# A decoder trunk on one core: the first MLP's scale and shift loaded one channel tile at a time, in four pieces

## The chip, the cores and the metric

The kernel runs on one core of one Trainium2 chip. The core has five engines with an instruction queue each: TensorE (PE) multiplies matrices into PSUM, VectorE (DVE) and ScalarE (ACT) work on vectors, GpSimd (POOL) does almost nothing here, and SyncE (SP) issues nearly all transfers from memory. Instructions of one engine start in the order in which they stand in its queue; engines wait for each other by semaphores. The metric is the device time of one execution in microseconds (us), lower is better.

## The reference, cut to what matters

```python
D_MODEL, SEQ, DEPTH, D_FF = 1024, 256, 2, 4096

def modulate(h, shift, scale):
    return h * (1 + scale[:, None, :]) + shift[:, None, :]

def squared_relu_mlp(h, w_up, w_down):
    a = jax.nn.relu(h @ w_up)
    return (a * a) @ w_down

c_act = jax.nn.silu(c)
for i in range(DEPTH):
    mod = c_act @ w_mod[i] + b_mod[i]                 # 1024 -> 6 * 1024
    sh1, sc1, g1, sh2, sc2, g2 = jnp.split(mod, 6, axis=-1)
    h = modulate(rmsnorm(x, norm_mix[i]), sh1, sc1)
    y = pool_mixer(...) if i == 0 else moba_attention(...)
    x = x + g1[:, None, :] * y
    h = modulate(rmsnorm(x, norm_mlp[i]), sh2, sc2)   # the change: sh2 and sc2 of layer 0
    x = x + g2[:, None, :] * squared_relu_mlp(h, w_up[i], w_down[i])
return rmsnorm(x, norm_final)
```

All arithmetic is float32. The shift `sh2` and the scale `sc2` of layer 0 have 1024 values each, and each value is a product of the 1024 numbers `c_act` with a column of `w_mod[0]`: 8 MB of weights are read for these two vectors.

## The kernel before, in words

Channels lie on the 128 partitions, so 1024 channels are 8 **channel tiles** k = 0 to 7, and the residual is kept as `xs[k]`, 128 by 256. The two layers run one after the other; the change touches the first MLP (names `m0u` for up, `m0d` for down) and the work just ahead of it.

**The up projection.** It has 32 outputs n by 8 inputs k, 256 weight tiles of 128 by 128. A load of 1 MB, `raw_w_j`, brings 16 tiles (128 by 2048 numbers), and is used in two **halves** of 8 tiles. Half h is split into two rounded parts so that a product keeps float32 accuracy: ScalarE rounds it (`split_hi`, line 247, `w_hi`), VectorE subtracts (`split_lo`, line 252, `w_lo`). Four buffers hold the halves, so half h + 4 waits for TensorE to be done with half h. A tile is three matmuls: `w_hi` by the high input, `w_hi` by the low input, `w_lo` by the high input (lines 271, 272, 273). For the first 14 outputs the order is input by input (`UP_ORDER`, `G_UP0 = 14`): 14 tiles for k = 0, then 14 for k = 1, and so on, 112 tiles in all, tile numbers 0 to 111. After them come the 18 other outputs, tiles 112 to 255. Tiles 0 to 7 are issued together (`mm_sums`, line 279).

**The inputs.** Input k is `h01_k`: `u` is the residual times the gain `gs01` (from the scale) times the row norm (line 648, VectorE), the high part is `u` plus the shift, rounded (line 654, ScalarE), the low part is the rest (line 657, VectorE). The gain needs the scale of tile k, the high part its shift.

**Scale and shift.** They come in two ways. *By TensorE* (`pair_mm`, `take`): the loaded weights are the moving operand and `c_act` the weights, and VectorE picks the wanted column out of PSUM (`pair_out`, line 325, output `pk`). *By VectorE* (`mod_dve`, line 295): the transposed weights are multiplied by the row `cact` and summed along the row into one column, 1024 wide, one instruction a channel tile. Before, `mlp0` brings scale and shift of tiles 0 and 1 ahead of the first MLP matmul (2 MB, by TensorE). The later scale tiles come in pairs by VectorE (`("m", 0, 4, j)`), the shift of tiles 2 to 5 by TensorE (`shift1`, `shift2`), that of tiles 6 and 7 by VectorE. Each pair gives two inputs at once.

**What sets the order.** The program is recorded in the order of the Python code. `load_order` lists the transfers, `issue` emits the next of them, each time a buffer was used up. All of these loads share five buffers of 1 MB (`raw`). A second ring of 32 buffers of 256 KB (tag `al`) holds temporaries of the first mixer and then the up projection's outputs. `head(d, ...)` puts work in front of tile d of the up projection: the splits of halves 2 to 11 and the inputs of the later pairs stand there by hand. From half 12 on, `next_tile` splits half h + 3 in front of tile 8h.

**Ahead of the MLP**, the gate of the first mixer (`g10`, the last of its weights) lets `pool_out` finish the residual, squares are summed on TensorE (`pool_sum`, line 390), `n1.rstd` makes the norm on ScalarE and VectorE, `take("mlp0", 0)` and `take("mlp0", 1)` follow, `R1` spreads the norm, and `keep_warm` puts matmuls with unused results in between.

Of the kernel before, what the change touches and what calls it, by code (L numbers as in the profile page):

```python
# [139 lines left out]
def tile_hybrid_pool_moba(  # L140
# [127 lines left out]

# [33 lines left out]

    def pair_mm(name, i, region):
# [3 lines left out]
        cols = slice(0, 64) if whole else slice(0, P)  # L309
        for k in range(nk):  # L310
            c0 = k if whole else i * nk + k
            for q in range(4):
                nc.tensor.matmul(
                    region[32 * q : 32 * q + 32, cols], ccol[:, c0 : c0 + 1].to_broadcast([P, 32]), w[:, k, q],
                    start=c0 == 0, stop=c0 == KD - 1, skip_group_check=True,
                )
        issue()

    def pair_out(name, i, region):
        key = PAIRS[name][i]  # L320
        layer, m, j = key
        base = 0 if name in BY_VECTOR else 64 * i
        for a in range(2):
            t = tmp.tile([P, 32], F32, tag="pk", bufs=4, name="pk")
            nc.vector.scalar_tensor_tensor(
                t, region[:, base + a * 32 : base + (a + 1) * 32], mod_bias(*key)[:, a : a + 1], pick,
                op0=ALU.add, op1=ALU.mult, accum_out=mods[layer, m][:, 2 * j + a : 2 * j + a + 1],
            )
        known.add(key)

    def mod(*key):
        for a in range(2):
            mod_dve(key, a)
            yield
# [842 lines left out]
```

## Time and profile before

| | us |
|---|---|
| median of three runs | 546.38 (546.02 to 546.96) |
| the profiled execution, its own time | 546.91 |
| its span in the profile | 545.1 |
| first matmul of the first MLP (from the span's start) | 52.27 |
| first matmul of its down projection | 145.8 |

Busy shares of the span: PE 98%, DVE 76%, ACT 59%. The profile is one execution; its time is 0.53 us above the median, and its span leaves 1.8 us of that time outside. A busy share says how long instructions of an engine were under way. Times below count from the start of the span.

### The profile page before, as it was taken

The page shows a single profiled execution, that of the slowest core. Times are in us where ns is not written, and L with a number is a line of the kernel's source. Part 1 is how long each engine was busy: PE and PEld are TensorE (multiplying, and loading weights), DVE is VectorE, ACT ScalarE, POOL GpSimd, SP SyncE. Part 2 cuts the span into 40 slices and gives each one's busy share as a digit, 9 for nine tenths or more (in the row PEclk, how much of TensorE's full clock was granted, in tenths as well). Part 3 has the DMA queues.
Part 4 walks back from the last instruction along what each step waited for, and adds up shares of the span by engine and source line. Part 5 has one row for each costly group of instructions (what it writes and reads, how often), then busy time and mean ns, then how long its engine had stood idle before and what let it go on. Part 6 is the DMA issues. An engine that isn't in the chain of part 4 may idle for free.

```text
span 545.1 us, 10988 instructions
## 1 busy us (share of the span) xinstructions
PE 533.8 (98%) x4424; PEld 496.4 (91%) x4424; DVE 413.1 (76%) x834; ACT 323.9 (59%) x605; POOL 2.5 (0%) x18
## 2 busy tenths in 40 slices
PE   8989999999999999999999999999999999999995
PEld 7767999999988888999999999999999998888895
DVE  1856997799889889957999994777887786765541
ACT  4224427789644455446988777666988774445531
POOL 1000000000000000000000000000000000000000
PEclk9998999999999999999999999999999999999998
DMA  8999999468999989964567874344555567576002
GB/s 330 416 419 415 388 393 361 156 243 313 331 354 409 382 315 343 337 228 151 217 213 285 290 286 171 124 188 154 167 222 182 206 231 265 219 266 255 0 1 77
DMA packets 22338, 140.41 MB, mean 258 GB/s; under 512 B 2416, under 2 KB 4608, under 8 KB 5904
## 3 DMA queue, kind: packets, MB, share of 16 engines
q1 hardware_dynamic: 22048, 138.61, 68.0%
q10 hardware_dynamic: 144, 1.05, 0.5%
q8 instruction: 34, 0.56, 0.4%
q14 instruction: 16, 0.13, 0.1%
q0 software_dynamic: 96, 0.06, 0.0%
HBM read 138.64 MB, written 1.07 MB: 256 GB/s over the span
## 4 chain that ended last, share of the span: by engine, by line
PE 87%; DMA 6%; DVE 3%; ACT 2%; issue 1%; DVEq 0%; ACTq 0%
PE m1d L264 9%; PE m0d L264 9%; PE m0u L271 5%; PE m0u L273 5%; PE m0u L272 5%; PE m1u L271 5%; PE m1u L272 5%; PE m1u L273 5%; PE m0d L265 5%; PE m1d L265 5%; PE qkv L271 5%; PE qkv L272 4%; PE qkv L273 4%; DMA raw_c_sh<-in_w_mod 3%; DMA raw_c_g<-in_w_mod 3%; PE sc L940 1%
## 5 line engine op out<-in xcount | busy, mean ns | idle before, releaser
L252 DVE TENSOR_TENSOR w_lo<-raw_w,w_hi 128x1024 fp32r<-128x1024 f32 x160 | 194.5, 1223 | 60.5 <-ACT w_hi L247 58.8
L247 ACT CAST w_hi<-raw_w 128x1024 fp32r<-128x1024 f32 x160 | 166.6, 1047 | 80.1 <-PE m1d L264 24.7
L264 PE MATMUL m1d<-m1u_al,w_hi 128*128 128x512 f32 x224 | 78.2, 393 | 0.0
L264 PE MATMUL m0d<-m0u_al,w_hi 128*128 128x512 f32 x224 | 78.0, 392 | 0.0
L295 DVE SCALAR_TENSOR_TENSOR raw_m<-raw_m,cact 128x1024 f32<-128x1024 f32 x64 | 77.6, 1217 | 0.0
L271 PE MATMUL m1u<-h_raw,w_hi 128*128 128x258 f32 x256 | 72.8, 284 | 0.0
L272 PE MATMUL m1u<-h_raw,w_hi 128*128 128x256 f32 x256 | 72.6, 284 | 0.0
L273 PE MATMUL m1u<-h_raw,w_lo 128*128 128x258 f32 x256 | 72.5, 283 | 0.0
L271 PE MATMUL m0u<-h,w_hi 128*128 128x256 f32 x248 | 69.7, 281 | 0.0
L273 PE MATMUL m0u<-h,w_lo 128*128 128x256 f32 x248 | 69.5, 280 | 0.0
L272 PE MATMUL m0u<-h,w_hi 128*128 128x256 f32 x248 | 69.3, 280 | 0.0
L265 PE MATMUL m1d<-m1u_al,w_lo 128*128 128x256 f32 x224 | 62.8, 280 | 0.0
L265 PE MATMUL m0d<-m0u_al,w_lo 128*128 128x256 f32 x224 | 62.7, 280 | 0.0
L271 PE MATMUL qkv<-h_raw,w_hi 128*128 128x258 f32 x192 | 57.4, 299 | 0.0
L272 PE MATMUL qkv<-h_raw,w_hi 128*128 128x256 f32 x192 | 54.6, 284 | 0.0
L273 PE MATMUL qkv<-h_raw,w_lo 128*128 128x258 f32 x192 | 54.4, 284 | 0.0
L264 PEld LDWEIGHTS m1d<-m1u_al,w_hi 128*128 128x128 f32 x224 | 42.1, 188 | 9.6
L264 PEld LDWEIGHTS m0d<-m0u_al,w_hi 128*128 128x128 f32 x224 | 42.0, 188 | 9.4
L273 PEld LDWEIGHTS m1u<-h_raw,w_lo 128*128 128x128 f32 x256 | 48.8, 191 | 0.0
L271 PEld LDWEIGHTS m1u<-h_raw,w_hi 128*128 128x128 f32 x256 | 48.7, 190 | 0.0
L272 PEld LDWEIGHTS m1u<-h_raw,w_hi 128*128 128x128 f32 x256 | 48.5, 190 | 0.0
L271 PEld LDWEIGHTS m0u<-h,w_hi 128*128 128x128 f32 x248 | 46.7, 188 | 0.6 <-issue 0.4
(182 smaller groups left out, 989.2 us busy)
## 6 DMA issues: line engine op xcount, KB each, us to landing
raw_w<-in_w_all SPq DMA_DIRECT2D x79, 1024.0 KB, 5.6
raw_m<-in_w_mod SPq DMA_DIRECT2D x32, 1024.0 KB, 6.4
raw_c_sh<-in_w_mod SPq DMA_DIRECT2D x8, 1024.0 KB, 13.8
raw_c_g<-in_w_mod SPq DMA_DIRECT2D x4, 1024.0 KB, 13.5
raw_c_mlp<-in_w_mod SPq DMA_DIRECT2D x2, 1024.0 KB, 11.6
raw_c_shift<-in_w_mod SPq DMA_DIRECT2D x2, 1024.0 KB, 8.0
T<-bd SPq DMA_DIRECT2D x8, 256.0 KB, 10.0
x<-in_xT ACTq DMA_DIRECT2D x1, 1024.0 KB, 5.9
```

The source lines that it names most:

```text
L247: nc.scalar.copy(hi, raw)
L252: nc.vector.tensor_sub(lo, raw, hi.bitcast(F32))
L264: nc.tensor.matmul(b, hi, hl[:, : 2 * S], start=start, stop=False)
L265: nc.tensor.matmul(b[:, S:], lo, hl[:, :S], start=False, stop=stop)
L271: nc.tensor.matmul(dst, hi, xh, start=start, stop=False)
L272: nc.tensor.matmul(dst[:, :S], hi, xl, start=False, stop=False)
L273: nc.tensor.matmul(dst, lo, xh, start=False, stop=stop)
L295: nc.vector.scalar_tensor_tensor(raw[:, a], raw[:, a], 1.0, cact, op0=ALU.mult, op1=ALU.mult, accum_out=dst[:, a : a + 1])
L940: nc.tensor.matmul(self.sc[e][:, t * P : t * P + n], self.qk[rows, 0, t * P : (t + 1) * P], self.qk[rows, 1, S - n :], start=True, stop=True,)
```

## The change

The scale and the shift of one channel tile k are now one load of 1 MB, the chunk `ml` k: 128 scale values and 128 shift values. It is not loaded into one of the five `raw` buffers but as four pieces of 128 by 512 (256 KB each) into four of the `al` buffers. The loads alternate: chunk k, then weight load k. Chunks 0, 1 and 4 are packed for TensorE (`ML_PE`, `take_ml`), the five others for VectorE (`ml_dve`): four row sums of 512, two for the scale and two for the shift, then an addition of the halves of each, then the bias. The inputs are made one at a time (`Input(k)`), and `head_work` places their parts and the splits of halves 1 to 17 by a rule in place of the list by hand. The code's line numbers shift: after the change the parts of a weight tile are made in lines 251 and 256, `u` in 681, the high part in 686, the low part in 690, the row sums in 302, and the three matmuls of a tile are in lines 274 to 276. In the head, `fold(7, 5)` and `pool_sum(7)` move behind `pool_out(0)`.

```diff
-PAIRS |= {f"mlp{j}": ((0, 4, j), (0, 3, j)) for j in range(1)}
-PAIRS |= {f"shift{j}": ((0, 3, j),) for j in (1, 2)}
...
+ML = ((0, 3), (0, 4))
+ML_PIECES = 4
+ML_SLOT = [16 + k if k < 4 else 8 + k for k in range(KD)]
+ML_PE = (0, 1, 4)
...
-HEAD_STEPS = 12
+HEAD_STEPS = 18
...
-    pair("mlp0")
-    order.extend([("w0a",), ("w0b",), ("w", 1)])
-    order.extend([("m", 0, 4, 1), ("c", "shift1", 0), ("w", 2), ("w", 3), ("m", 0, 4, 2), ("c", "shift2", 0)])
-    order.extend([("w", 4), ("m", 0, 4, 3), ("m", 0, 3, 3), ("w", 5)])
+    order.extend([("ml", 0), ("w0a",), ("w0b",)])
+    for k in range(1, KD):
+        order.append(("ml", k))
+        order.append(("w", k))
+    order.append(("w", KD))
...
+        elif key[0] == "ml":
+            n = TPC * P // ML_PIECES
+            t = [al_tile([P, n], f"ml{key[1]}_{i}") for i in range(ML_PIECES)]
+            for i in range(ML_PIECES):
+                nc.sync.dma_start(t[i], w_mod[0, ML_SLOT[key[1]]][:, i * n : (i + 1) * n])
...
+    def row_sum(raw, act_row, out):
+        nc.vector.scalar_tensor_tensor(raw, raw, 1.0, act_row, op0=ALU.mult, op1=ALU.mult, accum_out=out)
...
+    def ml_dve(k):
+        h = ML_PIECES // 2
+        n = D // h
+        t = tmp.tile([P, 2, h], F32, tag="ml", name=f"mlsum{k}")
+        for i, raw in enumerate(loaded["ml", k]):
+            a, b = divmod(i, h)
+            row_sum(raw, cact[:, b * n : (b + 1) * n], t[:, a, b : b + 1])
+        nc.vector.tensor_add(t[:, :, 0], t[:, :, 0], t[:, :, 1])
+        bias = vec[:, V_BMOD + ML[0][1] * KD : V_BMOD + (ML[0][1] + 2) * KD].rearrange("p (a b) -> p a b", a=2)
+        nc.vector.tensor_add(both_ml[:, :, k], t[:, :, 0], bias[:, :, k])
+        known.update(m + (k,) for m in ML)
...
+    def take_ml(k):
+        n = KD // ML_PIECES
+        for i, t in enumerate(loaded["ml", k]):
+            w = t.rearrange("p (k q n) -> p k q n", k=n, q=4)
+            columns_mm(w, i * n, 64, n, region[f"ml{k}"], i == 0, i == ML_PIECES - 1)
...
     pool_out(1)
-    fold(7, 5)
     take("g10", 1)
     given("g10", 1)
     pool_out(0)
-    pool_sum(7)
+    fold(7, 5)
     keep_warm(1)
     pool_sum(3)
     pool_sum(2)
+    keep_warm(1)
+    pool_sum(7)
     pool_sum(1)
...
-    take("mlp0", 0)
-    take("mlp0", 1)
-    both_given("mlp0")
+    take_ml(0)
+    ml_given(0)
...
-    head(2, splits(2))
-    head(6, splits(3))
-    head(7, mods_of(4, 1))
-    head(14, take_late("shift1", 0), lambda: given("shift1", 0), inputs(1))
-    head(18, splits(4))
...
+    def head_work():
+        ins = {k: Input(k) for k in range(1, KD)}
+        order = sorted(
+            [(G_UP0 * k, "in", k) for k in range(1, KD)] + [(HALF * h, "w", h) for h in range(1, HEAD_STEPS)]
+        )
+        highs = []
+        held = []
+
+        def give(k):
+            if k in ML_PE:
+                ml_given(k)
+            else:
+                ml_dve(k)
+            ins[k].gain()
+            ins[k].scaled(R1)
+
+        for need, kind, x in order:
+            at = need - HALF + 1 - max(0, 4 * (x - 13))
+            if kind == "in":
+                if x in ML_PE:
+
+                    at = max(at, HALF)
+                    head(max(at - 5, HALF), lambda x=x: region.update({f"ml{x}": bank(f"pm{x}")[:, :P]}), lambda x=x: take_ml(x))
+                if held:
+                    head(at, held.pop())
+                head(at, lambda x=x: give(x))
+                if x in ML_PE:
+                    head(at, ins[x].high, ins[x].low)
+                else:
+                    highs.append(ins[x].high)
+                    held.append(ins[x].low)
+            else:
+                def both(x=x, highs=tuple(highs)):
+                    w = split_hi(x)
+                    for high in highs:
+                        high()
+                    split_lo(x, *w)
+
+                highs.clear()
+
+                head(43 if x == 7 else at, both)
+                if held:
+                    head(at, held.pop())
+        assert not held
```

Three places in the queues show it. In the rows, `h01_u2` is `u` of input 2, `h01_2` its low part, `w4_lo` the low part of weight half 4, and numbers behind a name are the buffers'.

VectorE around input 2, before: halves 2 and 3, the sums of the scale of tiles 2 and 3, their shift from PSUM, both inputs, then half 4.

```order
L252 TENSOR_TENSOR w2_lo_728<-raw_w_1_567,w2_hi_726 128x1024
L252 TENSOR_TENSOR w3_lo_734<-raw_w_1_567,w3_hi_732 128x1024
L295 SCALAR_TENSOR_TENSOR raw_m_0_4_1_615,mod0_4_118<-raw_m_0_4_1_615,cact_107 128x1024 x2
L299 TENSOR_TENSOR mod0_4_118<-mod0_4_118,vec_80 128x2
L325 SCALAR_TENSOR_TENSOR pk_824,mod0_3_117<-pmc_789,vec_80 128x32
L325 SCALAR_TENSOR_TENSOR pk_826,mod0_3_117<-pmc_789,vec_80 128x32
L358 SCALAR_TENSOR_TENSOR gs0_4_696<-mod0_4_118,vec_80 128x2
L648 SCALAR_TENSOR_TENSOR h01_u2_829<-x_82,gs0_4_696,n1_R_717 128x256
L648 SCALAR_TENSOR_TENSOR h01_u3_831<-x_82,gs0_4_696,n1_R_717 128x256
L657 SCALAR_TENSOR_TENSOR h01_2_833<-h01_u2_829,mod0_3_117,h01_2_833 128x256
L657 SCALAR_TENSOR_TENSOR h01_3_835<-h01_u3_831,mod0_3_117,h01_3_835 128x256
L252 TENSOR_TENSOR w4_lo_853<-raw_w_2_686,w4_hi_851 128x1024
```

VectorE at the same place after the change.

```order
L256 TENSOR_TENSOR w2_lo_847<-raw_w_1_494,w2_hi_845 128x1024
L256 TENSOR_TENSOR w3_lo_877<-raw_w_1_494,w3_hi_875 128x1024
L302 SCALAR_TENSOR_TENSOR ml2_0_496,mlsum2_901<-ml2_0_496,cact_107 128x512
L302 SCALAR_TENSOR_TENSOR ml2_1_497,mlsum2_901<-ml2_1_497,cact_107 128x512
L302 SCALAR_TENSOR_TENSOR ml2_2_498,mlsum2_901<-ml2_2_498,cact_107 128x512
L302 SCALAR_TENSOR_TENSOR ml2_3_499,mlsum2_901<-ml2_3_499,cact_107 128x512
L321 TENSOR_TENSOR mlsum2_901<-mlsum2_901 128x2
L323 TENSOR_TENSOR both_ml_126<-mlsum2_901,vec_80 128x2
L377 SCALAR_TENSOR_TENSOR gs0_4_738<-both_ml_126,vec_80 128x1
L681 SCALAR_TENSOR_TENSOR h01_u2_909<-x_82,gs0_4_738,n1_R_754 128x256
L256 TENSOR_TENSOR w4_lo_927<-raw_w_2_529,w4_hi_923 128x1024
L690 SCALAR_TENSOR_TENSOR h01_2_925<-h01_u2_909,both_ml_126,h01_2_925 128x256
```

One input takes the place of two, four sums of 512 and two additions that of two sums of 1024, one addition and the two picked columns, and half 4 now stands between `u` and the low part of input 2; input 3 has a group of its own, later.

TensorE from the last gate weights (`raw_c_g`) to the two unused products ahead of the first MLP matmul, before.

```order
L313 MATMUL pma<-raw_c_g_1_412,ccol 32x64 x32
L390 MATMUL n_rms<-ones,n_sq_521 128x1 x2
L343 MATMUL junk<-fill 128x256
L390 MATMUL n_rms<-ones,n_sq_577 128x1 x2
L390 MATMUL n_rms<-ones,n_sq_580 128x1 x2
L390 MATMUL n_rms<-ones,n_sq_623 128x1 x2
L390 MATMUL n_rms<-ones,n_sq_626 128x1 x2
L343 MATMUL junk<-fill 128x256
L313 MATMUL pmb<-raw_c_mlp_0_432,ccol 32x128 x16
L313 MATMUL pmb<-raw_c_mlp_1_476,ccol 32x128 x16
L411 MATMUL n_rms<-vec,n_r 128x128 x2
L343 MATMUL junk_700<-fill 128x256 x2
```

TensorE at the same place after the change.

```order
L362 MATMUL junk<-fill 128x256
L409 MATMUL n_rms<-ones,n_sq_618 128x1 x2
L409 MATMUL n_rms<-ones,n_sq_621 128x1 x2
L362 MATMUL junk<-fill 128x256
L409 MATMUL n_rms<-ones,n_sq_554 128x1 x2
L409 MATMUL n_rms<-ones,n_sq_671 128x1 x2
L409 MATMUL n_rms<-ones,n_sq_674 128x1 x2
L362 MATMUL junk<-fill 128x256
L331 MATMUL pmb<-ml_0_415,ccol 32x64 x8
L331 MATMUL pmb<-ml_1_416,ccol 32x64 x8
L331 MATMUL pmb<-ml_2_417,ccol 32x64 x8
L331 MATMUL pmb<-ml_3_418,ccol 32x64 x8
```

The scale and shift products are half as wide (64 columns in place of 128, in four pieces of 8), the sum of tile 7 (`n_sq_521`, now `n_sq_554`) moved behind those of tiles 3 and 2, and one more unused product stands there.

SyncE's transfers from the MLP's first modulation weights on, before.

```order
L204 DMA raw_c_mlp0_0_432<-in_w_mod 128x2048
L204 DMA raw_c_mlp0_1_476<-in_w_mod 128x2048
L193 DMA raw_w_0_503<-in_w_all 128x1024
L196 DMA raw_w_0_503<-in_w_all 128x1024
L204 DMA raw_w_1_567<-in_w_all 128x2048
L204 DMA raw_m_0_4_1_615<-in_w_mod 128x2048
L204 DMA raw_c_shift1_0_668<-in_w_mod 128x2048
L204 DMA raw_w_2_686<-in_w_all 128x2048
L204 DMA raw_w_3_723<-in_w_all 128x2048
```

SyncE's transfers at the same place after the change.

```order
L200 DMA ml0_0_415<-in_w_mod 128x512
L200 DMA ml0_1_416<-in_w_mod 128x512
L200 DMA ml0_2_417<-in_w_mod 128x512
L200 DMA ml0_3_418<-in_w_mod 128x512
L192 DMA raw_w_0_441<-in_w_all 128x1024
L195 DMA raw_w_0_441<-in_w_all 128x1024
L200 DMA ml1_0_444<-in_w_mod 128x512
L200 DMA ml1_1_445<-in_w_mod 128x512
L200 DMA ml1_2_446<-in_w_mod 128x512
L200 DMA ml1_3_447<-in_w_mod 128x512
L208 DMA raw_w_1_494<-in_w_all 128x2048
L200 DMA ml2_0_496<-in_w_mod 128x512
```

Chunk 0 (1 MB) stands where `mlp0` (2 MB) stood, so the first weights follow 1 MB earlier, and from there on chunks and weight loads alternate.

## Rows read from the trace of the kernel before

**Rows 1.** Stretches: length, busy PE, PEld, DVE, ACT, POOL; PEclk, DMA share, GB/s.
```profile
0.00:52.20 52.20, 47.36 (x662) 37.74 (x662) 27.67 (x119) 15.75 (x32) 1.99 (x17) 0.97 0.98 394
52.20:545.10 492.90, 486.49 (x3762) 458.62 (x3762) 385.43 (x715) 308.16 (x575) 0.49 (x1) 1.00 0.66 243
```

**Rows 2.** Chain that ended last, 46 to 52 us: start, duration (us), what.
```profile
46.20 0.54 PE junk L343 x2
46.73 3.49 PE pmb L313 x64
...
50.24 0.77 DVE pk L325 x8
...
51.19 0.49 DVE h_u L648
...
51.71 0.52 ACT h L654
...
52.27 3.14 PE m0u L279 x24
```

**Rows 3.** Two stretches of 1 us before the first MLP matmul (PEclk: granted clock).
```profile
49.00:50.00 1.00, 1.00 (x24) 0.73 (x16) 0.00 (x0) 0.00 (x0) 0.00 (x0) 0.50 0.97 393
50.00:51.00 1.00, 1.00 (x10) 0.85 (x7) 0.76 (x9) 0.00 (x0) 0.00 (x0) 0.88 1.00 401
```

**Rows 4.** TensorE timeline (ninth tile, late take), then the down projection's first group.
```profile
55.25 0.28 PE L271 MATMUL m0u<-h,w_hi 128*128 128x256 f32 x1
...
57.57 1.10 PE L313 MATMUL pmc<-raw_c_shift,ccol 128*32 128x64 f32 x64
...
L264 PE MATMUL m0d<-m0u_al,w_hi x224: 387/392/402, 145.8 to 223.5; 128*128 128x512 f32 x112
```

**Rows 5.** VectorE timeline: start, duration (us), line, operation, out<-in, shape.
```profile
34.94 0.69 DVE L502 SCALAR_TENSOR_TENSOR pd<-win,ph 128x512 f32<-128x512 f32 x1
35.55 0.15 DVE L506 TENSOR_TENSOR pe<-win,vec 128x2 f32<-128x2 f32 x1
...
46.60 0.15 DVE L402 RECIPROCAL n_y<-n_s 128x2 f32<-128x2 f32 x1
46.79 0.16 DVE L404 TENSOR_TENSOR n_q<-n_y 128x2 f32<-128x2 f32 x1
...
54.19 3.49 DVE L252 TENSOR_TENSOR w_lo<-raw_w,w_hi 128x1024 fp32r<-128x1024 f32 x3
...
58.74 1.22 DVE L295 SCALAR_TENSOR_TENSOR raw_m<-raw_m,cact 128x1024 f32<-128x1024 f32 x1
...
60.00 0.16 DVE L299 TENSOR_TENSOR mod<-mod,vec 128x2 f32<-128x2 f32 x1
...
60.42 0.16 DVE L358 SCALAR_TENSOR_TENSOR gs<-mod,vec 128x2 f32<-128x2 f32 x1
60.61 0.88 DVE L648 SCALAR_TENSOR_TENSOR h_u<-x,gs,n_R 128x256 f32<-128x256 f32 x2
61.68 0.89 DVE L657 SCALAR_TENSOR_TENSOR h<-h_u,mod,h 128x256 fp32r<-128x256 f32 x2 [0.19 <-ACT h L654]
```

**Rows 6.** Costliest groups on the page: ScalarE's rounding of the weights.
```profile
L247 ACT CAST w_hi<-raw_w 128x1024 fp32r<-128x1024 f32 x160 | 166.6, 1047 | 80.1 <-PE m1d L264 24.7
```

**Rows 7.** VectorE: halves 18 and 24 of the weights; then a stretch of 10 us.
```profile
98.68 1.23 DVE L252 TENSOR_TENSOR w_lo<-raw_w,w_hi 128x1024 fp32r<-128x1024 f32 x1 [1.58 <-ACT w_hi L247]
...
120.75 1.22 DVE L252 TENSOR_TENSOR w_lo<-raw_w,w_hi 128x1024 fp32r<-128x1024 f32 x1
...
120.00:130.00 10.00, 10.00 (x87) 10.00 (x87) 9.72 (x17) 9.84 (x21) 0.00 (x0) 1.00 0.84 301
```

**Rows 8.** DMA: 4 us of the head; then issues: KB each, median us to landing.
```profile
36.00:40.00 4.00, 3.66 (x70) 2.64 (x72) 2.10 (x13) 0.77 (x2) 0.00 (x0) 1.00 1.00 418
...
wp<-in_w_pool SPq DMA_DIRECT2D x4, 256.0 KB, 14.3
...
out<-y SPq DMA_DIRECT2D x4, 256.0 KB, 2.4
```

More of the change, by code (lines that the diff above doesn't have):

```diff
@@ L308, in pair_mm, with picked @@
         w = loaded["c", name, i].rearrange("p (k q n) -> p k q n", k=nk, q=4)
[L309 to L316, printed above, removed]
-        issue()
+        columns_mm(w, 0 if whole else i * nk, 64 if whole else P, nk, region, whole or i == 0, whole or i == 1)
+        issue()
+    def picked(region, base, out):
+        t = tmp.tile([P, 32], F32, tag="pk", bufs=4, name="pk")
+        nc.vector.scalar_tensor_tensor(
+            t, region[:, base : base + 32], mod_bias(*out), pick, op0=ALU.add, op1=ALU.mult, accum_out=mod_col(*out)
+        )
+        known.add(out)
     def pair_out(name, i, region):
-        key = PAIRS[name][i]
-        layer, m, j = key
-        base = 0 if name in BY_VECTOR else 64 * i
+        layer, m, j = PAIRS[name][i]
         for a in range(2):
[L324 to L334, printed above, removed]
+            picked(region, (0 if name in BY_VECTOR else 64 * i) + 32 * a, (layer, m, 2 * j + a))
     junk = [bank("junk")]
@@ L355, in gain @@
     def gain(layer, m, v0, g, j0=0, j1=KD):
-        assert all((layer, m, j) in known for j in range(j0 // 2, j1 // 2))
+        assert all((layer, m, j) in known for j in range(j0, j1))
         v = v0 + layer * KD
@@ L362, in modv @@
     def modv(layer, m, k=None):
-        assert all((layer, m, j) in known for j in (range(4) if k is None else (k // 2,))), (layer, m)
+        assert all((layer, m, j) in known for j in (range(KD) if k is None else (k,))), (layer, m)
         return mods[layer, m]
@@ L548, in both_given, with ml_given @@
             given(name, i)
+    def take_ml(k):
[3 more added lines that the diff above has]
+            columns_mm(w, i * n, 64, n, region[f"ml{k}"], i == 0, i == ML_PIECES - 1)
+    def ml_given(k):
+        for a in range(2):
+            picked(region[f"ml{k}"], 32 * a, ML[a] + (k,))
     rms.rstd()
@@ L828, in head @@
         later(d, run)
-    def mods_of(m, j):
-        return lambda: weave(mod(0, m, j))
-    def splits(*hs):
-        return lambda: [split(h) for h in hs]
-    def take_late(name, half):
-        def run():
-            if name not in region:
-                region[name] = bank("pmc")[:, :P]
-            take(name, half)
-        return run
-    def inputs(j):
-        return lambda: Input(j).all(R1)
     first = Input(0)
@@ L1119, with by_tile @@
     wm = asf(by_row)
+    def by_tile(m, k):
+        return w_mod[0][:, m * D + k * P : m * D + (k + 1) * P]
+    for k, slot in enumerate(ML_SLOT):
+        both = np.concatenate([by_tile(m, k) for _, m in ML], axis=1)
+        if k in ML_PE:
+            wm[0, slot] = both.reshape(KD, P, 2, 4, 32).transpose(1, 0, 3, 2, 4).reshape(P, 2 * D)
+        else:
+            wm[0, slot] = both.T.reshape(2, P, D).transpose(1, 0, 2).reshape(P, 2 * D)
     for name, keys in PAIRS.items():
```

102 lines of the change are left out of this document (47 added, 55 removed).

## The prediction

> **What bounds the kernel now.** I read the busy times by stretch first. Behind 52.2 us TensorE is busy 486.5 of 492.9 us, and transfers take 0.66 of the engines' time; ahead of it transfers are saturated (share 0.98) [rows 1]. So the program is a head that loads modulation weights, then one long run of matmuls: what moves the end is when that run starts, and whether a matmul in it waits. The chain of waits gives the start: the last unused product behind the sums of squares (46.20), the `mlp0` products (46.73, 3.49 us), four picked columns (0.77), `u`, the high part, first MLP matmul at 52.27 [rows 2]. From tile 8 on the matmuls follow each other: tile 8 starts at 55.25, the down projection at 145.8, two late products of 1.1 us lie between, so a tile takes (145.8 - 55.25 - 2.2)/248 = 0.356 us, and 14 tiles, one input's worth, 4.98 us [rows 4]. TensorE therefore sets a pace of 4.98 us an input and 2.85 us a weight half. The other view to read is VectorE's timeline, for its work must keep that pace and it starts its instructions strictly in the order of its queue.
>
> **Head.** `take_ml(0)` has half as many columns to pass through TensorE: 3.49/2 = 1.75 us in place of 3.49, at the halved clock (0.50, the 1.2 GHz level) under which `mlp0` ran [rows 2, 3]. Bounds: 1.1 us, as the same shape took at full clock [rows 4], and 2.2, twice that. Two picks in place of four save 0.38. The moved fold and sum give nothing by my reckoning: the three sums that stand last still need the last square, and one more unused product stands in a gap. So the products start at 46.73 as before and end at 48.48; two picks, 0.39, and then 1.25 us as between 51.02 and 52.27 give the first MLP matmul at 50.1, **-2.1 us** (-1.65 to -2.75). The first weight half must be rounded by then: it lands 1 MB, 2.5 us at 418 GB/s, earlier [rows 8], and its subtraction stands ahead of the low part, a wait below 0.1 us.
>
> **Transfers.** The bytes are the same 8 MB, in an order that alternates. At 418 GB/s a chunk and a weight load land every 5.0 us, from chunk 1 at some 49 us: chunk k lands about 5 us before its input is due, and the ring of 32 buffers is free by then (its old tiles belong to the first mixer, done by 46.2). I cost the pieces at nothing. A 256 KB load among the 1 MB loads of the head took 14.3 us from issue to landing, nearly all of it waiting in line, while the rate stayed at 418 GB/s; one alone took 2.4 us [rows 8]. The Trainium skill ("DMA: Bandwidth & Descriptors", Anatomy of one DMA) gives each transfer a fixed 2.0 us besides its bytes, for the software path; paid in full by every piece that would be 4 x 2.6 us a chunk. The rate in line speaks against paying it here, and the rival below prices it.
>
> **VectorE's load an input.** Prices [rows 5]: an operation 512 wide lasts 0.69 us and the next starts 0.61 after it (34.94, 35.55); a subtraction of a half lasts 1.22 and holds the queue 1.14 (three in 3.49); `u` and low part 0.49 each, 0.40 apart; a small operation that needs the one before starts 0.20 after it (46.60, 46.79), and `u` 0.19 after the gain (60.42, 60.61); an addition starts 0.04 after the sum's end (58.74 + 1.22, 60.00). The row sum of 512 isn't in the trace; the product of 512 at line 502, same operation and width without the sum, is the nearest row, and at 1024 the sum (1.22) costs what the subtraction costs, so I take 0.61. By VectorE an input then costs: three sums 1.83; the fourth's end and the addition 0.73; bias, gain and `u` 0.20 + 0.20 + 0.19; `u` 0.40; a half 1.14; the low part with what follows it 0.45; the second half 1.14: **6.3 us against TensorE's 4.98**. I walked the queues with a half's rounding at 1.05 us on ScalarE [rows 6] and get 6.37 with the hand-overs. Before, a pair (9.96 us of TensorE) costs at most two scale and two shift sums (4.6), four halves (4.6) and 2.5 for the inputs: 11.7 once, 9.4 for the pairs whose shift TensorE makes, with halves 1 to 3 and inputs 0 and 1 done before the pace begins. Now only input 0 is there.
>
> **Walk from 50.15** (time of the wait on TensorE, then what it waits for). Input 1: chunk products end at 54.2, `u` 54.9, high part 56.0, low part 56.55; tile 14 is reached at 56.35 and its second matmul waits 0.2. Half 2 is rounded only behind the high part (55.9 to 56.95, the order of ScalarE) and subtracted by 58.2; tile 16 waits 0.8 for it. Input 2: half 3 holds VectorE until 59.25, the sums begin there, `u` 62.5, high part 63.55; tile 28 is reached at 62.25 and waits 1.3, then its second matmul waits 0.87 more, since half 4's subtraction stands between `u` and the low part. Input 3 comes 6.37 us later, TensorE 4.98: 1.4 (0.53 + 0.87). Input 4 is by TensorE (VectorE: two picks in place of the sums) and wins the time back: no wait. Input 5 just arrives. Inputs 6 and 7 cost 1.3 and 1.4. Sum **+7.3 us** by tile 112. Each wait that TensorE takes is one that VectorE doesn't win back, as its queue is full. Bounds: 5.0 if the sums and hand-overs are a tenth cheaper; 8.9 if nothing on VectorE overlaps, so that each sum holds it 0.69 (0.32 for each of five chunks, 1.6). On the second the Trainium skill speaks ("VectorE: DVE Perf Modes", The DRAIN you can't avoid): the next operation doesn't start until the pipe is empty. By it this term would be 8.9 and the time 554.2. The rows disagree, 0.61 against 0.69, and I go by them.
>
> **Tiles 112 to 255.** Here VectorE is busy 9.7 of 10 us before the change too [rows 7], so a lost lead isn't won back. Half 18 is done at 98.68 + 1.23 = 99.9, its third matmul is due at 55.25 + 2.2 + 136 x 0.356 + 0.24 = 106.1: a lead of 6.2. Half 24 is done at 121.97 and due at 123.2, a lead of 1.2. After the change tile 144 is due at 111.2 (50.15 + 2.98 + 2.1 + 136 x 0.356 + 7.3 + 0.24) and half 18, by the same walk, done at 107.4 (halves 14 to 17 each wait for a rounding that stands behind the first outputs on ScalarE): lead 3.8, 2.4 less. So half 24 is 1.2 late; **+1.0 us** (0 to 2.4). Behind that nothing is touched.
>
> **Sum.** -2.1 + 7.3 + 1.0 = +6.2: from the profiled execution's 546.91 to 553.1. It lies 0.53 above the median 546.38, so I predict **552.6 us**, 1.1% slower.
>
> **Rivals.**
> *VectorE keeps up* (not slower). Place: the five chunks of row sums. If a sum held VectorE for s in place of 0.61, an input costs 3.9 + 4s: 4.98 at s = 0.27. At s = 0.38 the waits of inputs 2 and 3 and of 6 and 7 shrink to the opening's 1.0 and about 1.5 for low parts: -2.1 + 2.5 = +0.4, 546.8, the same. Below 0.27 some 1.0 is left: -2.1 + 1.0, 545.3, which is where faster begins. Rows 5 speak against it, a 512-wide float32 operation at 0.61; for it speaks only that the sum itself isn't in the trace.
> *The clock.* Ahead of the MLP TensorE's clock fell to 0.50 and was at 0.88 in the stretch from 50 to 51, behind 3.49 us of `mlp0` products [rows 3]. With half of these and gaps around them it may rise later, and the first 24 passes (3.14 us, [rows 2]) would take up to twice as long at the lower level; half of that is +1.6, 554.2. The waits of 1 to 2 us at each input could bring it down once more, at like cost.
> *Pieces pay alone.* If every piece cost 2.4 us by itself, as the lone store did [rows 8], a chunk and a load would take 4 x 2.4 + 2.5 = 12.1 us in place of 5.0 for seven inputs: +50, some 595. The rate in line speaks against it.
> *Nothing overlaps on VectorE*: the upper bound of the walk, 8.9 in place of 7.3, 554.2; the rows that show 0.61 and 1.14 against lengths of 0.69 and 1.22 speak against it.
> *The waits are halved*: the low parts' 0.87 are hidden, or the walk counts hand-overs twice: 3.6 + 0.5 - 2.1 = +2.0, 548.4, still slower.
>
> **How the numbers follow.** Forecast 0.62; clock 0.10; waits halved 0.09; nothing overlaps 0.04; pieces 0.02; VectorE keeps up 0.13, of which 0.07 the same and 0.06 faster. A measurement of this kernel tells a difference of about 0.2% (1.1 us) from no change. Lower end of the forecast: -2.75 + 5.0 + 0 = 548.6; upper end: -1.65 + 8.9 + 2.4 = 556.0. The range 548.0 to 556.5 takes both in, with the halved waits and the clock, and leaves out the case in which VectorE keeps up, the pieces and the outermost combinations.
>
> **What would show it.** Right: first MLP matmul near 50.1; row sums of 512 some 0.61 apart; TensorE's waits at lines 274 and 275 for the high and low parts of inputs 2, 3, 6, 7, and at 276 for half 2; VectorE busy over 9 of 10 us from 57 to 95; the down projection's first matmul near 152 in place of 145.8. Wrong: no such waits (VectorE cheaper than its rows), waits for chunks themselves (transfers), or a granted clock of 0.50 behind 51 us.

## The result, and the profile after

The changed kernel takes **553.11 us** (median of 4 runs, 552.98 to 554.81) against 546.67 for the kernel before on the same chip (4 runs, 546.02 to 547.75): ratio 1.0123, 95% interval 1.0097 to 1.0149. The forecast was 552.6 in a range of 548.0 to 556.5. One thing has to be known to read the numbers below: ahead of the MLP TensorE's granted clock fell to 0.50 (its 1.2 GHz level) in some of the profiled executions and stayed at 1.00 in others, and where it fell the first MLP matmul comes 1 us or more later (50.13 in experiment 2 against 49.12 in experiment 5). It fell in the profile of before [rows 3] and not in that of after.

Three stretches of the profiled execution of after (553.14 us, span 551.3), cut at the first MLP matmul and at the first matmul of the down projection; columns as in [rows 1].

```profile
0.00:49.00 49.00, 45.84 (x664) 36.19 (x664) 27.65 (x115) 15.73 (x32) 2.05 (x17) 1.00 0.98 391
49.00:151.70 102.70, 98.27 (x899) 95.04 (x900) 87.96 (x174) 61.72 (x114) 0.50 (x1) 0.98 0.79 297
151.70:551.30 399.60, 393.23 (x2866) 366.46 (x2864) 302.95 (x577) 246.08 (x460) 0.00 (x0) 1.00 0.62 227
```

Before, the same cuts stand at 52.27 [rows 2] and 145.8 [rows 4], with the end at 545.1. So the head is 3.2 us shorter (49.02 against 52.27), the up projection 9.2 longer (102.7 against 93.5), and behind it the two agree within 0.3 (399.6 against 399.3). In the middle stretch TensorE is idle for 4.4 us; before it had no such wait. The idle time is less than the 9.2 us because a matmul counts as busy for 0.28 us although the next one starts after 0.12 when nothing holds it, and because time at a low clock counts as busy too.

The head, on TensorE's timeline (start, duration, line, operation; in brackets the idle time before it and what ended that), and the clock while the chunk's products ran:

```profile
46.05 1.10 PE L331 MATMUL pmb<-ml,ccol 128*32 128x64 f32 x64
...
49.02 2.21 PE L282 MATMUL m0u<-h,w_hi 128*128 128x256 f32 x16 [0.36 <-ACT h L686]
```
```profile
46.00:47.00 1.00, 1.00 (x65) 0.94 (x64) 0.63 (x5) 0.81 (x1) 0.00 (x0) 1.00 1.09 432
```

The products take 1.10 us at clock 1.00, where `mlp0` took 3.49 at 0.50 [rows 2, 3]. They also start 0.7 us earlier than before (46.05 against 46.73). So does the work that leads up to them: the products of the last gate weights start as soon as these have landed, first before, then after the change.

```profile
41.74 1.10 PE L313 MATMUL pma<-raw_c_g,ccol 128*32 128x64 f32 x64
```
```profile
40.99 1.10 PE L331 MATMUL pma<-raw_c_g,ccol 128*32 128x64 f32 x64
```

In the variants of the changed kernel below, the gate's products start anywhere from 40.79 (experiment 6) to 41.95 (experiment 11), so the 0.7 us is not shown to come from the change.

VectorE through one input (chunk 2, half 4, low part, half 5, and the first sum of chunk 3):

```profile
58.22 0.69 DVE L302 SCALAR_TENSOR_TENSOR ml<-ml,cact 128x512 f32<-128x512 f32 x1
...
58.83 0.69 DVE L302 SCALAR_TENSOR_TENSOR ml<-ml,cact 128x512 f32<-128x512 f32 x1
...
60.78 0.16 DVE L321 TENSOR_TENSOR mlsum<-mlsum 128x2 f32<-128x2 f32 x1
60.98 0.16 DVE L323 TENSOR_TENSOR both_ml<-mlsum,vec 128x2 f32<-128x2 f32 x1
61.17 0.16 DVE L377 SCALAR_TENSOR_TENSOR gs<-both_ml,vec 128x1 f32<-128x1 f32 x1
61.37 0.49 DVE L681 SCALAR_TENSOR_TENSOR h_u<-x,gs,n_R 128x256 f32<-128x256 f32 x1
61.77 1.22 DVE L256 TENSOR_TENSOR w_lo<-raw_w,w_hi 128x1024 fp32r<-128x1024 f32 x1
62.91 0.48 DVE L690 SCALAR_TENSOR_TENSOR h<-h_u,both_ml,h 128x256 fp32r<-128x256 f32 x1
63.37 1.23 DVE L256 TENSOR_TENSOR w_lo<-raw_w,w_hi 128x1024 fp32r<-128x1024 f32 x1
64.51 0.68 DVE L302 SCALAR_TENSOR_TENSOR ml<-ml,cact 128x512 f32<-128x512 f32 x1
```

From the first sum of one chunk to that of the next it is 64.51 - 58.22 = 6.29 us, without a hole, where TensorE needs 4.98. A sum lasts 0.69 and the next starts 0.61 after it, the two numbers that the prediction took from another line. The Trainium skill ("VectorE: DVE Perf Modes", The DRAIN you can't avoid) has the next operation start only when the pipe is empty, and adds that one that is not held starts earlier; the rows here show the earlier start, 0.61 against a length of 0.69.

What TensorE does meanwhile. A matmul starts 0.12 us after the one before it; a larger distance between two starts is a wait.

```profile
56.35 0.28 PE L275 MATMUL m0u<-h,w_hi 128*128 128x256 f32 x1
57.22 0.39 PE L276 MATMUL m0u<-h,w_lo 128*128 128x256 f32 x1 [0.58 <-DVE w_lo L256]
...
61.23 0.28 PE L276 MATMUL m0u<-h,w_lo 128*128 128x256 f32 x1
62.45 0.38 PE L274 MATMUL m0u<-h,w_hi 128*128 128x256 f32 x1 [0.95 <-ACT h L686]
63.44 0.38 PE L275 MATMUL m0u<-h,w_hi 128*128 128x256 f32 x1 [0.61 <-DVE h L690]
...
85.91 0.28 PE L276 MATMUL m0u<-h,w_lo 128*128 128x256 f32 x1
86.20 0.39 PE L274 MATMUL m0u<-h,w_hi 128*128 128x256 f32 x1
87.19 0.38 PE L275 MATMUL m0u<-h,w_hi 128*128 128x256 f32 x1 [0.60 <-DVE h L690]
...
92.00 0.28 PE L276 MATMUL m0u<-h,w_lo 128*128 128x256 f32 x1
92.50 0.39 PE L274 MATMUL m0u<-h,w_hi 128*128 128x256 f32 x1 [0.21 <-ACT h L686]
93.48 0.39 PE L275 MATMUL m0u<-h,w_hi 128*128 128x256 f32 x1 [0.60 <-DVE h L690]
...
127.51 0.28 PE L275 MATMUL m0u<-h,w_hi 128*128 128x256 f32 x1
128.55 0.39 PE L276 MATMUL m0u<-h,w_lo 128*128 128x256 f32 x1 [0.76 <-DVE w_lo L256]
```

These are, in order, half 2, inputs 2, 6 and 7, and half 24. Input 3, due at 68, shows no wait, because TensorE itself was slow then (windows of 1 us; the clock is the third number from the end):

```profile
64.00:65.00 1.00, 1.00 (x10) 1.00 (x9) 1.00 (x2) 0.28 (x1) 0.00 (x0) 0.87 1.02 404
65.00:66.00 1.00, 1.00 (x7) 1.00 (x6) 1.00 (x5) 0.00 (x0) 0.00 (x0) 0.50 1.02 404
```

Behind the waits of input 2 the clock stood at 0.50 for some 3 us; 15 matmuls took 68.04 - 64.84 = 3.20 us in place of 1.77, and these 1.4 us are as long as the wait that they cover.

**A trap in the chain of waits.** Followed back from its end, the chain runs over VectorE and ScalarE from 128 to 73 us, and ahead of that over transfers:

```profile
48.68 9.23 DMA ml<-in_w_mod
...
67.02 6.39 DMA ml<-in_w_mod
73.43 1.05 ACT w_hi L251
74.50 1.23 DVE w_lo L256
```

That reads as if chunks were late. But at 73.43 ScalarE had just come free (a high part ran from 73.02 and holds the queue some 0.4); the transfer that landed at 73.41 only won by a hair. No matmul waits for a transfer in this stretch. Which of the two it is, experiment 6 decides.

### The profile page after: what moved, and what is told of

Read it like the earlier page. It is cut to its first block, busy times and chain, and to the rows that moved or that the text cites. A ratio compares the mean times of both kernels' runs of the same rounds, so it can differ in the third digit from the quotient of the medians.

```text
span 551.3 us, 11065 instructions
## 1 busy us (share of the span) xinstructions
PE 537.4 (97%) x4426; PEld 497.7 (90%) x4426; DVE 418.6 (76%) x864; ACT 323.5 (59%) x605; POOL 2.5 (0%) x18
## 4 chain that ended last, share of the span: by engine, by line
PE 77%; DMA 12%; DVE 6%; ACT 3%; issue 1%; SPq 0%; DVEq 0%; ACTq 0%
PE m0d L268 9%; PE m1d L268 9%; DMA ml<-in_w_mod 6%; PE m1u L274 6%; PE m1u L275 6%; PE m1u L276 6%; PE m0d L269 5%; PE m1d L269 5%; PE qkv L274 5%; PE qkv L275 4%; PE qkv L276 4%; DMA raw_c_sh<-in_w_mod 3%; DVE w_lo L256 2%; ACT w_hi L251 2%; DMA raw_w<-in_w_all 2%; PE m0u L276 1%
## 5 line engine op out<-in xcount | busy, mean ns | idle before, releaser
L275 PE MATMUL m0u<-h,w_hi 128*128 128x256 f32 x248 | 70.6, 285 | 1.8 <-DVE h L690 1.8
L274 PE MATMUL m0u<-h,w_hi 128*128 128x256 f32 x248 | 71.0, 286 | 1.3 <-ACT h L686 1.2
L276 PE MATMUL m0u<-h,w_lo 128*128 128x256 f32 x248 | 70.8, 285 | 1.3 <-DVE w_lo L256 1.3
L302 DVE SCALAR_TENSOR_TENSOR raw_m<-raw_m,cact 128x1024 f32<-128x1024 f32 x56 | 68.2, 1218 | 0.0
L274 PEld LDWEIGHTS m0u<-h,w_hi 128*128 128x128 f32 x248 | 47.6, 192 | 2.7 <-ACT h L686 1.8
L275 PEld LDWEIGHTS m0u<-h,w_hi 128*128 128x128 f32 x248 | 47.5, 191 | 2.5 <-DVE h L690 2.4
L276 PEld LDWEIGHTS m0u<-h,w_lo 128*128 128x128 f32 x248 | 47.4, 191 | 2.1 <-DVE w_lo L256 1.9
```

The source lines that it names most:

```text
L274: nc.tensor.matmul(dst, hi, xh, start=start, stop=False)
L275: nc.tensor.matmul(dst[:, :S], hi, xl, start=False, stop=False)
L276: nc.tensor.matmul(dst, lo, xh, start=False, stop=stop)
L302: nc.vector.scalar_tensor_tensor(raw, raw, 1.0, act_row, op0=ALU.mult, op1=ALU.mult, accum_out=out)
```

## Experiments

Theory **load**: VectorE's work an input, 6.3 us against TensorE's 4.98, makes TensorE wait. Rival **transfers**: the chunks in four pieces arrive late. For the shorter head, theory **gap**: the moved sum closes a hole on TensorE and keeps its clock up; rival **arrival**: it does nothing. Each ratio is to the kernel before on the same chip: 545.89 us in experiments 1 to 4 and again in 10 and 11, 545.97 in 5 to 8, 546.26 in 9.

**1. The moved sum alone, in the kernel before.**
```diff
     pool_out(1)
-    fold(7, 5)
     take("g10", 1)
     given("g10", 1)
     pool_out(0)
-    pool_sum(7)
+    fold(7, 5)
     keep_warm(1)
     pool_sum(3)
     pool_sum(2)
+    keep_warm(1)
+    pool_sum(7)
```


> The kernel before with one edit alone: the fold and the sum of squares of tile 7, with one unused product, stand where the change puts them (fold behind the last mixer outputs, sum behind the sums of tiles 3 and 2). Theory 'gap': in the kernel before TensorE stood idle for 0.56 us at 43.40, and its clock was at 0.50 from 47 to 50 us; with the move there is work in that gap and the clock stays at 1.00, so the mlp0 products last about 1.75 us in place of 3.49, and the first MLP passes and the start of the up projection come 1.7 to 2.3 us earlier: about 544.5 us against 546.7. Rival 'arrival': the earlier head of the changed kernel comes from the order of its loads or from the earlier end of the chunk's products alone, and the moved sum changes nothing, as the prediction had it: 546.5 us and the clock at 0.50 from 47 to 50 us as before.


Measured: 546.66 us against 545.89, ratio 1.0011 (1.0002 to 1.0021). In its profile the clock stayed at 1.00 and the first MLP matmul came 1.7 us earlier than in the profile of before:
```profile
46.49 1.95 PE L313 MATMUL pmb<-raw_c_mlp,ccol 128*32 128x128 f32 x64
...
50.54 2.18 PE L279 MATMUL m0u<-h,w_hi 128*128 128x256 f32 x16 [0.59 <-ACT h L655]
...
56.33 0.88 PE L313 MATMUL pmc<-raw_c_shift,ccol 128*32 128x64 f32 x48 [0.44 <-DMA raw_c_shift<-in_w_mod]
```
0.5 us of it went back to a load that was not there yet at 55.7. And the time is not better: the mean granted clock of its runs goes from 0.993 to 0.999, as that of the runs of before does. What the profile showed was one execution with the clock up, not the work of the moved sum.

**2. The sum put back, in the changed kernel** (the diff of experiment 1 the other way round).


> The changed kernel with the fold, the sum of tile 7 and the unused product put back to where the kernel before has them. Theory 'gap': TensorE idles some 0.5 us ahead of the sums, its clock falls to 0.50 before the chunk's products, these last 1.75 to 2.2 us in place of 1.10, the first MLP matmul comes at 50 to 50.5 us in place of 49.0, and the time rises by 1.0 to 1.5 us to about 554.4 us. Rival 'arrival': the clock stays at 1.00 all the same, and the time stays at 553.1 us.


Measured: 553.44 us, ratio 1.0142 (1.0129 to 1.0155). Its profile has the hole and the low clock:
```profile
42.67 0.58 PE L409 MATMUL n_rms<-ones,n_sq 128*128 128x1 f32 x4 [0.60 <-DVE n_sq L562]
...
45.93 1.93 PE L331 MATMUL pmb<-ml,ccol 128*32 128x64 f32 x64
...
50.13 2.21 PE L282 MATMUL m0u<-h,w_hi 128*128 128x256 f32 x16
```
Taken alone it would speak for "gap". But the profiles of experiments 3 and 7, which have the sum moved, show the clock at 0.50 at 46 us all the same (first MLP matmul at 50.61 and 50.72), and the time does not differ from that of the changed kernel by more than the intervals. And the mean clock of some runs of before, where the sum isn't moved, is 0.999. So the moved sum is not what keeps the clock up, and "gap" falls as an account of the time; whether the hole makes a fall more likely is not shown (it fell in both profiles with the sum in its old place, and in four of ten with the sum moved, experiment 4 left out), and what makes the clock fall in one execution and not in another stays open.

**3. The low part ahead of the subtraction.**
```diff
                     for high in highs:
                         high()
+                    for low in lows:
+                        low()
                     split_lo(x, *w)
```


> The changed kernel with the low part of an input issued on VectorE ahead of the second half's subtraction in place of behind it; nothing is added or taken away. Theory 'load': VectorE's work an input (6.3 us against TensorE's 4.98) is what makes TensorE wait, so the waits for low parts shrink from 0.87 to about 0.4 but the next input's wait grows by as much: 553 to 554 us, no gain. Rival 'order': the three waits of 0.87 us for low parts are lost only because a subtraction stands ahead of them; without it they go, 553.1 - 2.6 = 550.5 us.


Measured: 555.35 us, ratio 1.0176 (1.0163 to 1.0189): slower than either expected. The starts show where it went:
```profile
64.06 0.39 PE L274 MATMUL m0u<-h,w_hi 128*128 128x256 f32 x1 [0.95 <-ACT h L686]
64.58 0.39 PE L275 MATMUL m0u<-h,w_hi 128*128 128x256 f32 x1
...
70.94 0.38 PE L274 MATMUL m0u<-h,w_hi 128*128 128x256 f32 x1 [1.44 <-ACT h L686]
```
The low part of input 2 costs 0.52 - 0.12 = 0.40 in place of 0.87, and input 3 then waits 1.6 at its first matmul in place of some 0.4. "Order" falls, "load" holds: what is won at one instruction is lost at the next. By tile 43 the starts have lost 4.6 us against before, in experiment 5 below 4.5: no gain, and no loss either. The rest of the difference goes with the clock, which fell twice in this profile: ahead of the first MLP matmul (46 to 48 us; it comes at 50.61) and behind input 3 (72 to 75 us).

**4. Half of the sums left out.**
```diff
         for i, raw in enumerate(loaded["ml", k]):
             a, b = divmod(i, h)
+            if b == 1:
+                continue
...
-        nc.vector.tensor_add(t[:, :, 0], t[:, :, 0], t[:, :, 1])
```


> The changed kernel with two of the four row sums of each of the five chunks that VectorE sums left out, and the addition that joins the halves (so the scale and shift of these chunks hold the sum of half their terms). Every transfer stays. Theory 'load': an input costs VectorE some 6.3 - 1.2 - 0.1 = 5.0 us, TensorE's pace; the waits of inputs 3, 6 and 7 go and that of input 2 shrinks from 2.1 to about 0.7, 4 to 5 us less: 548.0 to 549.0 us. Rival 'transfers': the waits come from chunks that land late or in pieces; then they stay, 552 to 553 us.


Measured: 560.11 us, ratio 1.0262. The run answers another question than it was made for. A square of the head waited for a chunk:
```profile
54.26 0.42 ACT L552 ACTIVATE n_sq<-x 128x256 f32<-128x256 f32 x1 [10.20 <-DMA ml<-in_w_mod]
```
Pieces and squares come from one ring of buffers. A piece that nobody reads has no reader to wait for: the square was given such a buffer and stood behind its transfer, which moved the whole program by 10 us. The stage itself did as "load" says (chunk to chunk 4.9 us; of the waits for inputs 2, 3, 6 and 7 one of 0.7 us is left, at the low part of input 2), but its chunks had 10 us more lead, so it doesn't decide.

**5. The changed kernel again**, as the mark for the next three.


> The changed kernel itself, unchanged, beside the next three on the same chip: the time that they stand against. Both theories: 553.1 us, 1.012 to 1.013 times the kernel before. Its first MLP matmul at 49.0 us if the clock stays at 1.00 ahead of it, at 50.1 to 50.6 us if it falls there, as it did in the profiles of two earlier runs.


Measured: 553.0 us, ratio 1.013 (1.0111 to 1.015). Here the clock stayed at 1.00 in the head and in the up projection, first MLP matmul at 49.12, and input 3 waits as forecast:
```profile
68.84 0.39 PE L274 MATMUL m0u<-h,w_hi 128*128 128x256 f32 x1 [0.21 <-ACT h L686]
69.83 0.39 PE L275 MATMUL m0u<-h,w_hi 128*128 128x256 f32 x1 [0.61 <-DVE h L690]
```
Its up projection lasts 102.5 us, that of the first profile 102.7: the low clock there had only taken the place of this wait.

**6. A quarter of each sum, every buffer read.**
```diff
-            row_sum(raw, cact[:, b * n : (b + 1) * n], t[:, a, b : b + 1])
+            row_sum(raw[:, :P], cact[:, b * n : b * n + P], t[:, a, b : b + 1])
```


> The changed kernel with each row sum of the five chunks that VectorE sums taken over the first 128 of its 512 columns (so scale and shift of these chunks hold a quarter of their terms); every buffer is still read, every transfer stays, and the instructions are as many. Theory 'load': a sum costs VectorE some 0.2 to 0.25 us in place of 0.61, an input 6.3 - 4 x 0.37 = 4.8 us, below TensorE's 4.98: the waits of inputs 2, 3, 6 and 7 go (2.1, 1.5, 1.1 and 1.4 us), those for halves 2 and 24 stay: 547 to 548.5 us. Rival 'transfers': the waits come from chunks that land late or in pieces, 552 to 553 us.


Measured: 548.0 us (546.86 to 550.84), ratio 1.0038 (1.0022 to 1.0055), 5.0 us less than the changed kernel. VectorE, one input:
```profile
58.02 0.29 DVE L302 SCALAR_TENSOR_TENSOR ml<-ml,cact 128x128 f32<-128x128 f32 x1
...
62.73 0.29 DVE L302 SCALAR_TENSOR_TENSOR ml<-ml,cact 128x128 f32<-128x128 f32 x1
```
4.71 us from chunk to chunk, below 4.98; of the waits for inputs 2, 3, 6 and 7 only 0.4 us is left. The first MLP matmul is at 48.82, the down projection starts at 145.61: 96.8 us in place of 102.5. Bytes and pieces are the same. "Transfers" falls.

**7. All chunks on TensorE.**
```diff
-ML_PE = (0, 1, 4)
+ML_PE = tuple(range(KD))
```


> The changed kernel with all eight chunks multiplied on TensorE (as chunks 0, 1 and 4 are) and none summed on VectorE. Theory 'load': the waits of inputs 2, 3, 6 and 7, 6.1 us in all, go; five times 64 products at 1.03 us cost TensorE 5.15 us; 0.5 to 1.5 us less than the changed kernel: 551.5 to 552.6 us. Rival 'transfers': the waits stay and the products come on top, 558 us.


Measured: 552.55 us, ratio 1.0123 (1.0104 to 1.0142). All waits of TensorE that the view lists from 49 to 152 us:
```profile
PE m0u L276 <- DVE w_lo L256: 0.8, 1, 0.8
PE m0u L282 <- ACT h L686: 0.2, 1, 0.2
```
No input is waited for any more, and the products eat up the gain, as expected: by the starts, each of the five further sets moves the next tile by 1.23 us. Half 24 is still waited for, though VectorE has no sums of chunks.

**8. Eight transfers a chunk.**
```diff
-                nc.sync.dma_start(t[i], w_mod[0, ML_SLOT[key[1]]][:, i * n : (i + 1) * n])
+                for b in range(2):
+                    c = slice(b * n // 2, (b + 1) * n // 2)
+                    nc.sync.dma_start(t[i][:, c], w_mod[0, ML_SLOT[key[1]]][:, i * n : (i + 1) * n][:, c])
```


> The changed kernel with every 256 KB piece of a chunk fetched as two transfers of 128 KB into the halves of its buffer: 32 transfers more in the same bytes. If a transfer in a full line costs nothing but its bytes, as the prediction had it: 553.1 us, no change. Rival 'pieces pay': if each costs even 0.3 us beside its bytes, a chunk and a load take 1.2 us longer than the 5 us at which they land now, and from chunk 2 on the row sums wait for chunks: 557 us or more.


Measured: 555.0 us, ratio 1.0164 (1.0143 to 1.0185), between the two. Transfers from 36 to 90 us, first of this kernel, then of experiment 5:
```profile
DMA packets 10584, 17.34 MB, mean 321 GB/s; under 512 B 1177, under 2 KB 9369, under 8 KB 9625
```
```profile
DMA packets 6449, 20.82 MB, mean 386 GB/s; under 512 B 713, under 2 KB 713, under 8 KB 5065
```
Pieces of 128 KB do cost rate. TensorE still waits for no chunk, and the up projection lasts 102.5 us as in experiment 5. What this profile loses against that one lies outside it: 1.0 us ahead of the first MLP matmul (50.15 against 49.12) and 0.4 behind the up projection. In this profile the clock fell at 12 and at 46 us, and its four runs have mean clocks of 0.990 to 0.994; whether the transfers cause that is open.

**9. GpSimd takes halves off VectorE.**
```diff
-        nc.vector.tensor_sub(lo, raw, hi.bitcast(F32))
+        (nc.gpsimd if h in BY_POOL else nc.vector).tensor_sub(lo, raw, hi.bitcast(F32))
...
+BY_POOL = (3, 5, 8, 10, 12, 20, 22)
...
-                head(43 if x == 7 else at, both)
+                head(43 if x == 7 else max(at - 7, 0) if x in BY_POOL else at, both)
```


> The changed kernel with the subtraction of seven weight halves (3, 5, 8, 10, 12, and 20 and 22 of the later tiles) on GpSimd in place of VectorE; the first five of them are issued seven tiles earlier, so that GpSimd has some 5 us for each. Nothing is left out. No run shows what a subtraction of 128 x 1024 takes on GpSimd: from below it is VectorE's 1.2 us, from above there is no row. Theory 'load': VectorE's work an input falls from 6.3 to 5.2 us, close to TensorE's 4.98: of the waits of inputs 2, 3, 6, 7 (6.0 us) and of half 24 (1.4 us) some 1.5 us stay, 547 to 549 us, if GpSimd takes less than 4 us a half and VectorE's own instructions keep their durations. Rivals: GpSimd takes longer than 5 us a half, or slows VectorE's instructions while it works, and TensorE waits for it instead: 553 us or more.


Measured: 559.38 us, ratio 1.0237 (1.0209 to 1.0265). GpSimd's first subtraction, and VectorE beside it:
```profile
56.92 2.49 POOL L257 TENSOR_TENSOR w_lo<-raw_w,w_hi 128x1024 fp32r<-128x1024 f32 x1 [45.05 <-ACT w_hi L252]
```
```profile
57.06 2.90 DVE L303 SCALAR_TENSOR_TENSOR ml<-ml,cact 128x512 f32<-128x512 f32 x1
```
The second rival: a sum that meets it lasts 2.90 us in place of 0.69, until GpSimd is done. Each of the first five subtractions holds one sum so (2.85 to 2.93); VectorE loses 2.2 us for the 1.14 it was to save, and the up projection lasts 108.8 us in place of 102.5. A sum that was already under way when GpSimd started kept its 0.69. The Trainium skill ("Advanced Engine Details and Errata", GPSIMD Details) says it: the engine shares a read and a write interface with VectorE and conflicts with instructions that have two inputs in SBUF, as a row sum has. The trace agrees.

**10. Halves 13 to 17 earlier.**
```diff
-            at = need - HALF + 1 - max(0, 4 * (x - 13))
+            at = need - HALF + 1
+            if kind == "w":
+                at -= max(0, min(16, 4 * (x - 12)))
```


> The changed kernel with the rounding of weight halves 13 to 17 issued earlier: a half's lead ahead of its tile grows by four tiles a half from half 13 on and reaches 23 tiles at half 16, in place of from half 14 on and reaching 23 at half 17; nothing else is moved. Theory 'late halves': half 24 is waited for (1.4 us) because halves 14 to 17 are rounded late, behind the first outputs, as the prediction's last term had it; with an earlier lead half 24 is there in time: 553.0 - 1.4 = 551.6 us. Rival 'waits hand it on': VectorE enters tile 112 late because of its row sums; then the wait for half 24 stays, 553.0 us.


Measured: 551.98 us, ratio 1.0107 (1.0089 to 1.0124), 1.0 less than experiment 5, but on another chip and with intervals that overlap. The trace says more. What is left of half 24's wait:
```profile
126.72 0.28 PE L275 MATMUL m0u<-h,w_hi 128*128 128x256 f32 x1
127.29 0.38 PE L276 MATMUL m0u<-h,w_lo 128*128 128x256 f32 x1 [0.29 <-DVE w_lo L256]
```
This is 0.57 - 0.12 = 0.45 and the 0.1 behind it. In all, the starts behind tile 112 lose 0.6 us against before, where experiment 5 loses 1.8. Experiments 6 and 7, with shorter sums and with none, lose the same 1.8 there. Together they settle the last term: the lead is lost by rounding halves late, not handed on by the row sums.

**11. Both.** Experiments 7 and 10 together, the lead growing from half 12 on (`x - 11` in place of `x - 12`).


> All eight chunks multiplied on TensorE, with the halves issued earlier (lead growing from half 12 on): no row sums of chunks on VectorE and no late halves. Theory 'load' with 'late halves': 552.5 less the 1.4 us of half 24 is 551.1 us, with no wait of TensorE in the up projection but that at its start; the five further products of 1.03 us are then what is left against the kernel before, besides a head that is 1.1 to 3.2 us shorter. Rival 'waits hand it on': with no row sums the wait for half 24 would have been gone already, which the run with all chunks on TensorE did not show.


Measured: 550.58 us (550.08 to 553.54), ratio 1.0089 (1.0066 to 1.0111). No wait of TensorE is left in its up projection. (The profiled execution is the slowest of the six, 553.54, with the clock at 0.50 from 46 to 52 us.) It is the best of the variants of the changed kernel that leave nothing out, and 4.7 us slower than the kernel before: the five further sets of products cost 1.23 us each by the starts, 6.2 in all, and the shorter head gives part of that back. No run points to one that beats both.

## Why the prediction was right, by its steps

**VectorE sets the pace: right, and shown.** 6.29 us an input against 6.3 by rows; the sum of 512 at 0.69 and 0.61. Less of it alone gives 5.0 us back (experiment 6), the same amount in another order gives none (3).

**The waits, +7.3 by tile 112: right.** Counted from the first MLP matmul, tile 112 starts 7.2 us later in experiment 5 than in the profile of before, and 7.3 later in the profile of after. In experiment 5, where no low clock covers any wait, these are the distances of starts less 0.12, with the 0.1 that the matmul behind a wait takes longer, against the forecast: half 2 0.85 (0.8); input 1 0.1 (0.2); input 2 2.08 (2.17); input 3 1.36 (1.4); inputs 4 and 5 none; input 6 1.14 (1.3); input 7 1.34 (1.4). Sum 6.9; the other 0.3 is spread thinly over many starts. VectorE was busy for 33.68 of the 38 us from 57 to 95, a little less than the 9 of 10 that the prediction named as a sign.

**Half 24, +1.0: mechanism right, size 1.8.** Half 24 is waited for by 1.4 us, and two shorter waits stand ahead of it, 0.2 for half 21 and 0.3 for half 23. (The working gives 1.2 for half 24 and then takes 1.0; 1.8 lies within its 0 to 2.4.) They are late by what experiments 6, 7 and 10 say. Together the waits are 9.0 against 8.3 forecast, and 9.0 is what the up projection of experiment 5 grew by, so none of its growth is left over.

**Head, -2.1: in the profiles -3.2.** The bound at full clock (-2.75) is passed as well. First, the clock: the term took the products at half of it, 1.75 us, and they took 1.10 at clock 1.00. At 0.50 they take 1.93 (experiment 2), and `mlp0`'s take 1.95 at 1.00 (experiment 1), so halving the width alone is worth 0.85 at the full clock. Second, the start: they began 0.7 earlier than in the profile of before, as the last gate weights had landed earlier, and the term took the start from one execution. Over the variants of the changed kernel the chunk's products start between 45.84 and 47.83 (experiment 4 left out). Where the clock did fall, experiment 2 has the first MLP matmul at 50.13, and the forecast was 50.1, but in other parts: products from 45.93 for 1.93, and then more time to the first matmul, since what stands between ran at the low clock too. The bounds should have had both clocks for the whole head. The pair of profiles also flatters the change: the medians of before and of experiment 5 differ by 7.0 us, and with 9.0 lost in the up projection that leaves an estimated 2 us for the head, close to the forecast.

**The clock after waits: a rival that came in part.** A granted clock of 0.50 behind 51 us was one of the prediction's signs of being wrong, and it came: behind input 2's waits, in the profiles of after and of experiments 9 and 10, and not in experiment 5. But it cost nothing net in the profile of after (up projection 102.7 against 102.5), since the time was lost to the next wait anyway; the rival would have added 1.6.

**Pieces at nothing: right for 256 KB in this kernel.** No matmul waits for a chunk. Experiment 8 shows that halving them again costs rate, so it isn't free at any size. The 2.4 us that the rival took for a piece by itself is the median of four stores that were under way together, issued 0.4 to 0.5 us apart, so no run shows what one costs alone.

The sum, +6.2 forecast, is +6.2 in the spans (551.3 against 545.1): the head was 1.1 better, the up projection 0.9 worse and the rest 0.3 worse. The pace and the waits were forecast by their mechanism; that the total meets the forecast so closely is luck, as these misses cancel.

## What to carry to other kernels

Work that is moved off the critical path in equal amounts still has to fit the pace of the stage into which it goes: add up the queue of the engine that takes it, by the distances of starts, for one period, and compare with the period. When it doesn't fit, reordering only moves the wait, and a second engine helps only if it can run beside the first. And read a stage's size from more than one execution when the clock at its start is not the same in all.

## What the runs showed of the hardware that was not expected

- A subtraction of 128 x 1024 on GpSimd takes 2.4 to 2.8 us, and a row sum on VectorE, with two inputs in SBUF, that starts while it runs stands still until it ends (0.69 becomes 2.9).
- TensorE's clock fell to 0.50 at about 46 us in the profiles of before and of experiments 2, 3, 7, 8 and 11, and stayed at 1.00 in those of after and of experiments 1, 5, 6, 9 and 10, with the same instructions around it in most of them. In experiment 4 it fell at 47, in the long wait of the head.
- With pieces of 128 KB among the 1 MB loads, a full line moved 321 GB/s over the stretch in which it moved 386 with pieces of 256 KB.
